# A two-layer decoder trunk on one core: rotary sine product a step later, first swaps by ScalarE, raw weights asked for later, scores of two query blocks in one bank each

## The chip, the cores and the metric

The kernel runs on one core of a Trainium2 chip. The metric is the device time of one execution in microseconds (us); the time before the change is the median of three runs, 1908.89 us (1908.52 to 1911.45).

## What is computed

Two layers, each of the same form, on 512 positions of width 1024; all weights are float32 and are read from HBM once:

```
h    = modulate(rmsnorm(x, norm_mix_g), sh_m, sc_m)          # sh, sc, g come from c by w_ada
proj = h @ w_in                                              # a_in, b_in, q, k, v, gate_pre
a    = silu(layernorm(conv31(glu(a_in))));  y_a = a @ w_a_out
y_b  = (bg * conv3(cg * xb)) @ w_b_out
q, k = rope(q), rope(k)        # [t1*cos - t2*sin, t2*cos + t1*sin] on halves of 32 of a head part of 64
for each of 8 heads, each block of 128 queries, both parts c of q and k:
    p_c = softmax(mask(q_c @ k_c.T * scale));   a = p_0 - lam * p_1;   o = a @ v
y_c  = rmsnorm(o, subln_g) * (1 - lambda_init) @ w_c_out
x    = x + g_m * ((sigmoid(gates) * (y_a, y_b, y_c) summed) @ w_out)
x    = x + g_f * (square(relu(modulate(rmsnorm(x), sh_f, sc_f) @ w_ff1)) @ w_ff2)
out  = rmsnorm(x, final_g)
```

## The kernel before

**Products.** Every float32 product is done as three reduced-precision products: an operand is split into a high part (ScalarE's cast, L394 for weights) and the rest (VectorE's subtraction, L402), and `proj` (L426) adds high*high, high*rest and rest*high in one PSUM bank. A product of 128 output columns has 24 matmuls of 512 columns.

**Order.** The program order of all engines is written by hand. `mm` (L143) counts the columns that TensorE has been given, and each 4096 columns are a **step**. Side work is written as generators: `spawn(g, d)` starts one d steps later, and `yield n` lets n steps go by, so the number of a step says only where in each engine's stream an instruction stands. Each engine then goes through its own stream in order and waits where its data aren't there. Tasks that are due in one step run in the order in which they were put off (the earlier first).

**Weights.** A raw tile is 1024 rows by 256 columns, 1 MB, and there are two of them (`wraw`, two buffers). `raw_issue` (L365) asks for the next one on SP's queue. `w_split` (L373) turns half a raw tile, a chunk, into high and rest: the cast, one step later the subtraction, and after a second half at once the next `raw_issue`. `release` starts the split of the chunk three ahead one step after a product has used its own chunk. In the attention part the chunks of a pair of heads come as q first half, k first half, q second half, k second half, then the two halves of v (each four row blocks by 256 columns).

**Rotary.** `rope` (L707): ScalarE copies the product from PSUM to an SBUF tile `t` (L712), four DMAs on SP's queue copy the four groups of 32 partitions to `sw` with neighbours swapped (L714), one step later VectorE multiplies by the cosine (L717), two steps after that it multiplies `sw` by the sine and adds (L719, L720); a step later ScalarE casts (L723, L724), a step later VectorE makes the rests (L728, L729 for q; L734 for k) and SP moves halves between partitions (L738, L739); two steps later the tile counts as there.

**Attention.** `heads` (inside `mixer`) starts a head every nine steps, the first when its q and k count as there and two steps have gone by. `attend` (L780) writes the scores of one query block every two steps. Both parts of a block have a PSUM bank of their own (`ps_s`, two banks in all), 128 to 512 columns in use. `softmax` (L745): a step later VectorE's masked minimum reads both banks (L754), a step later ScalarE's exponentials (L761), two steps later VectorE's combination (L766, L767, L770). Five steps after the last block TensorE transposes the weights (L806), in three portions a step apart, four steps after the last of them it multiplies by v (L817); then come ScalarE's copy (L821), a step later transposes of it (L825), and four small steps of the norm with a row broadcast (L455) and a multiplication by VectorE (L842).

**Where the steps fall.** Let V be the step at which the value products of one pair of heads end. The four q and k products of the next pair end at V+3, V+6, V+9 and V+12, its value products at V+18. Two casts of weights stand at V+4 (second halves of q and k), with their subtractions and the two requests for raw tiles (v of this pair, q of the next) at V+5; the cast of the first half of v stands at V+7, its subtraction at V+8. In layer 0 the even head's four blocks stand at V+1, V+3, V+5 and V+7, the odd head's from V+10 on; in layer 1 both two steps earlier. The tables of the sine and cosine are ready before the first product ends.

**The layers' first tiles.** In layer 0 the four products of the first pair are made by hand at the end of the list `START` (`first_product`), in layer 1 three of the four in `closing`, in the banks of `ps_mm` and `ps_s`. `lambdas` (L228) makes lam with small instructions; its product on TensorE (L251) stands two steps after VectorE's difference (L246).

Of the kernel before, what the change touches and what calls it, by code (L numbers as in the profile page):

```python
# [44 lines left out]
ADA_BR = 0  # L45
FIRST = 2
RWAIT = 2


RDELAY = (0, 1, 1)  # L50
# [17 lines left out]
SH_M, SC_M, G_M, SH_F, SC_F, G_F = range(6)  # L68
# [3 lines left out]
def kernel(  # L72
# [7 lines left out]
    nc = tc.nc  # L80
# [23 lines left out]
    def ftile(dt=F32, shape=None):  # L104
        return slot("f", dt, shape)
# [4 lines left out]
    def ps_s():  # L110
        return psum.tile([P, S], F32, tag="s", name=nm("s"), bufs=2)
# [119 lines left out]
    def lambdas():  # L231
        lq, lk = slot("at", F32, [1, L, 2, 64]), slot("at", F32, [1, L, 2, 64])
        for j, (a, b) in enumerate(((lam_q1, lam_k1), (lam_q2, lam_k2))):
            G.dma_start(lq[:, :, j, :], a[None, :, :])
            G.dma_start(lk[:, :, j, :], b[None, :, :])
        yield 15
        V.tensor_tensor(lq, lq, lk, op=ALU.mult)
        ls, le, ll = stile(4), stile(4), stile(2)
        V.tensor_reduce(out=ls[0:1, :], in_=lq.rearrange("p l j d -> p (l j) d"), op=ALU.add, axis=AX.X)
        ones = ftile(F32, [1, P])  # L240
        V.memset(ones, 1.0)
        yield 1
        A.activation(le[0:1, :], ls[0:1, :], AF.Exp)
        yield 1
        for l in range(L):
            V.scalar_tensor_tensor(  # L246
                out=ll[0:1, l : l + 1], in0=le[0:1, 2 * l + 1 : 2 * l + 2], scalar=-lam_init[l],
                in1=le[0:1, 2 * l : 2 * l + 1], op0=ALU.add, op1=ALU.subtract)
        yield 2
        pt = ps_t()  # L250
        T.matmul(pt[:, 0:2], ones, ll[0:1, :], start=True, stop=True)  # L251
        yield 1
        V.tensor_copy(nlam, pt[:, 0:2])
        written.add("lam")
# [103 lines left out]
            chunks += [(len(specs) + g, hh) for hh in range(2) for g in range(len(grp))]  # L358
            specs += grp
    raws, wready = [], []  # L360
    wnext, spare = [0], set()

    def raw_issue():
        if len(raws) < len(specs):
# [6 lines left out]
    def w_split(extra=None):  # L371


        if wnext[0] >= len(chunks):
            return
        n, hh = chunks[wnext[0]]
        wnext[0] += 1
        raw, kk = raws[n], specs[n][2]
        if kk < 0:

            shape, rs = [P, 4, 256], raw[:, 4 * hh : 4 * hh + 4, :]
            n_k = 4
        else:
            shape, rs = [P, 8, P], raw[:, :kk, hh * P : (hh + 1) * P]
            n_k = kk
        if extra:
            half = [P, n_k // 2] + shape[2:]
            his = [slot(extra, F32R, half) for _ in range(2)]
            parts = [(hf, rs[:, i * half[1] : (i + 1) * half[1], :]) for i, hf in enumerate(his)]
        else:  # L390
            hi = wpool.tile(shape, F32R, tag="wh", name=nm("wh"))
            parts = [(hi[:, :n_k, :], rs)]
        for h_, r_ in parts:
            A.copy(h_, r_)  # L394
        yield 1
        if extra:
            los = [slot(extra, F32R, half) for _ in range(2)]
        else:
            lo = wpool.tile(shape, F32R, tag="wl", name=nm("wl"))
            los = [lo[:, :n_k, :]]  # L400
        for l_, (h_, r_) in zip(los, parts):
            V.tensor_tensor(l_, r_, h_.bitcast(F32), op=ALU.subtract)  # L402
        wready.append(([h_[:, k, :] for h_, _ in parts for k in range(n_k // len(parts))],
                       [l_[:, k, :] for l_ in los for k in range(n_k // len(parts))], extra))
        if hh == 1:
            raw_issue()

    def getw():
# [295 lines left out]
    cos_t = const.tile([P, S], F32, name="cos_t")  # L704
    sin_t = const.tile([P, S], F32, name="sin_t")

    def rope(pp, res, j):  # L707

        t, sw = ftile(), ftile()
        A.copy(t, pp)  # L712
        for q in range(4):
            nc.sync.dma_start(sw[32 * q : 32 * q + 32, :], t[32 * (q ^ 1) : 32 * (q ^ 1) + 32, :])  # L714
        yield 1
        u = ftile()
        V.tensor_tensor(u, t, cos_t, op=ALU.mult)  # L717
        yield 2
        V.tensor_tensor(sw, sw, sin_t, op=ALU.mult)  # L719
        V.tensor_tensor(u, u, sw, op=ALU.add)  # L720
        yield 1
        d0, d1 = slot("qk", F32R), slot("qk", F32R)
        A.copy(d0, u)  # L723
        A.copy(d1[64:, :], u[64:, :])  # L724
        yield 1
        if j % 2 == 0:
            e0, e1 = slot("qk", F32R), slot("qk", F32R)
            V.tensor_tensor(e0, u, d0.bitcast(F32), op=ALU.subtract)  # L728
            V.tensor_tensor(e1[64:, :], u[64:, :], d1[64:, :].bitcast(F32), op=ALU.subtract)  # L729
            moves = ((d0, d0, d1, d1), (e0, e0, e1, e1))  # L730
            parts = (d0, d1, e0, e1)
        else:
            lo = u.bitcast(F32R)
            V.tensor_tensor(lo, u, d0.bitcast(F32), op=ALU.subtract)  # L734
            moves = ((d0, u, d1, u),)
            parts = (d0, d1)
        for a0, b0, a1, b1 in moves:
            nc.sync.dma_start(a0[64:, :].bitcast(F32), b0[:64, :].bitcast(F32))  # L738
            nc.sync.dma_start(a1[:64, :].bitcast(F32), b1[64:, :].bitcast(F32))  # L739
        yield RWAIT  # L740
        res.append(parts)
# [38 lines left out]
    def attend(l, hd, q, k, v, res):  # L780

        a = []
        l0 = stile(4)
        for i in range(NTB):
            n = (i + 1) * P
            sps = [ps_s(), ps_s()]
            blk = slice(i * P, (i + 1) * P)
            for cc in range(2):
                T.matmul(sps[cc][:, :n], q[cc][:, blk], k[cc][:, :n], start=True, stop=False)  # L789
                T.matmul(sps[cc][:, :n], q[2 + cc][:, blk], k[cc][:, :n], start=False, stop=True)  # L790
            spawn(softmax(l, i, sps, l0, a))
            yield QSTEP
        yield AWAIT

        tiles = [None] * NTB
        for js in ((0,), (1, 3), (2,)):
            pt = ps_t()
            off = 0
            hi, lo = slot("at", F32R) if js[0] < 2 else None, slot("at", F32R)
            w2 = 2 * P  # L800
            if js[0] == 2:
                hi, lo = lo[:, :w2], lo[:, w2:]
            for j in js:
                w = S - j * P
                for i in range(j, NTB):
                    T.transpose(pt[:, off + (i - j) * P : off + (i - j + 1) * P],  # L806
                                a[i][:, j * P : (j + 1) * P], ident)
                tiles[j] = (hi[:, off : off + w], lo[:, off : off + w])
                off += w
            spawn(weights_t(pt, off, hi, lo))  # L810
            yield 1
        yield PWAIT
        po = ps_t()
        for j in range(NTB):
            for i, (x_, y_) in enumerate(PASSES):
                c0 = j % 2 * 256 + hd % 2 * P
                T.matmul(po[:, j * P :], v[j // 2][x_][:, c0 : c0 + P], tiles[j][y_],  # L817
                         start=j == 0 and i == 0, stop=j == NTB - 1 and i == 2)
        yield 1
        of = slot("o")  # L820
        A.copy(of, po)  # L821
        yield 1
        pt = ps_t()
        for b in range(NTB):
            T.transpose(pt[:, b * P : (b + 1) * P], of[:, b * P : (b + 1) * P], ident)  # L825
        yield 1
        ss = stile(4)
        for b in range(NTB):
            A.activation(pt[:, b * P : (b + 1) * P], pt[:, b * P : (b + 1) * P], AF.Square,
                         scale=128.0**-0.5, accum_out=ss[:, b : b + 1])  # L830
        yield 4

        e = stile(4)
        G.tensor_tensor(e, l0, l0, op=ALU.mult)
        G.tensor_scalar(out=e, in0=e, scalar1=EPS, scalar2=None, op0=ALU.mult)
        G.tensor_tensor(e, e, ss, op=ALU.add)
        y = rsqrt_small(e, 4)
        yield 2
        rb = bcast(y, 4)
        yield 1  # L840
        assert (l, "sub") in written
        V.scalar_tensor_tensor(out=of, in0=of, scalar=subg[:, l : l + 1], in1=rb,  # L842
                               op0=ALU.mult, op1=ALU.mult)
        res[hd] = of


    def mixer(l, h, qk, nfirst):
# [15 lines left out]
                yield PERIOD  # L863

        spawn(heads())
        for hp in range(NH // 2):
            if hp:
                qk, nfirst = [], 0
# [162 lines left out]
        def branch(pp, br, e, tg):  # L1031
# [6 lines left out]
            else:  # L1038
# [2 lines left out]
                yield 1  # L1041
                yield from split(m[e], merged)

        for br, act in enumerate((oo, yb, ya)):
            hold[0] = False
            if br == ADA_BR and l == 0:
# [121 lines left out]
    h = new_h()  # L1168
# [111 lines left out]
    def first_product(qt, i):  # L1280
# [6 lines left out]
        proj(first[i], w1[i], h, 0, S, 2 * qt, 2 * qt + 2)  # L1287
        if qt == 3:
            release(w1[i])
            spawn(rope(first[i], qk, i))  # L1290
            run_due()

    def rows_scale(qt):
# [35 lines left out]
    for l in range(L):  # L1329
# [6 lines left out]
        f = mlp(l, h, f, NF)  # L1336
        if l + 1 < L:
            qk = []
            h = closing(l, G_F, f, l + 1, 0, lambda pp, i: rope(pp, qk, i))
    ending(f)  # L1340
    while tasks:
        step()
# [35 lines left out]
```

## Time and profile before

| | us |
|---|---|
| median of 3 runs | 1908.89 |
| lowest and highest | 1908.52, 1911.45 |
| profiled execution | 1904.28 |
| its span, first to last instruction | 1902.5 |

The profiled execution thus has 1.8 us around its span and is 4.6 us under the median of the runs. Its mean granted TensorE clock is 0.997 of full. The profile is one execution: for each instruction its engine, line, start and length, the idle time of the engine before it, and what ended that. A tile `raw` is a raw weight tile, `wh` and `wl` are high and rest of a chunk, `s` a bank of scores, `t` another small PSUM bank, `f` and `st` small SBUF tiles, `cv` (in this part) the softmax tiles. A DMA row on SP's queue (`SPq`) is the issue, not the transfer.

### The profile page before, as it was taken

To read this page: it belongs to the slowest core of one execution; us is meant where nothing else is said; L and a number is where in the kernel's file an instruction comes from. 1 tells how busy PE (TensorE), PEld (TensorE's weight loads), DVE (VectorE), ACT (ScalarE), POOL (GpSimd) and SP (SyncE) were. 2 spreads that over 40 slices of the span, in tenths; PEclk is the share of its full clock that TensorE was granted. 3 is DMA by queue.
4 is the path that set the end of the run, shared out by engine and by line. 5 is a ranking of instruction groups with operands and counts; after the bars stand their busy time and mean duration, and the time that the engine had idled before them with its cause. 6 is when DMAs were issued, how large, how long until landed. Compare 5 with 4: busy or idle time off the path is not lost.

```text
span 1902.5 us, 24972 instructions
## 1 busy us (share of the span) xinstructions
PE 1874.3 (99%) x9565; PEld 1599.9 (84%) x9565; DVE 1256.0 (66%) x2139; ACT 785.8 (41%) x1420; POOL 63.4 (3%) x109
## 2 busy tenths in 40 slices
PE   8999999999999999999999999999999999999998
PEld 6788888888889888888898888888888898888888
DVE  7788789996676556565677777898654563333336
ACT  4466652223333524333445666322243353424253
POOL 1011010000000000000000000000000000000000
PEclk9999999999999999999999999999999999999999
DMA  8644323444554455555535442232233422223221
GB/s 272 181 130 126 101 67 98 151 138 145 166 178 135 139 178 195 177 185 182 171 97 142 123 122 73 89 104 96 67 100 100 133 89 89 89 93 106 89 89 67
DMA packets 211527, 241.20 MB, mean 127 GB/s; under 512 B 10408, under 2 KB 178480, under 8 KB 211408
## 3 DMA queue, kind: packets, MB, share of 16 engines
q1 hardware_dynamic: 210480, 239.38, 40.6%
q8 instruction: 75, 1.23, 0.3%
q0 software_dynamic: 768, 0.23, 0.1%
q14 instruction: 44, 0.36, 0.1%
q10 hardware_dynamic: 160, 0.01, 0.0%
HBM read 216.50 MB, written 2.10 MB: 115 GB/s over the span
## 4 chain that ended last, share of the span: by engine, by line
PE 93%; DMA 3%; DVE 2%; issue 1%; SPq 1%; ACT 1%; POOL 0%; POOLq 0%; DVEq 0%; ACTq 0%
PE mm L145 83%; PE s L145 3%; DMA f<-f 2%; PE t L817 1%; PE s L789 1%; PE s L790 1%; PE t L806 1%; SPq L714 1%; PE t L1193 1%; PE t L455 0%; PE t L303 0%; PE t L825 0%; POOL st L438 0%; DVE f L719 0%; PE t L1214 0%
## 5 line engine op out<-in xcount | busy, mean ns | idle before, releaser
L145 PE MATMUL mm<-h,wh 128*128 128x512 f32 x2720 | 851.3, 392 | 0.0
L145 PEld LDWEIGHTS mm<-h,wh 128*128 128x128 f32 x2720 | 509.6, 188 | 103.3
L145 PE MATMUL mm<-h,wl 128*128 128x512 f32 x1360 | 533.6, 392 | 0.0
L394 ACT CAST wh<-raw 128x1024 fp32r<-128x1024 f32 (+1 forms) x308 | 308.9, 1005 | 407.2 <-PE mm L145 358.2
L402 DVE TENSOR_TENSOR wl<-raw,wh 128x1024 fp32r<-128x1024 f32 (+1 forms) x308 | 358.2, 1166 | 69.6 <-ACT wh L394 65.9
L145 PE MATMUL mm<-qk,wh 128*128 128x512 f32 (+1 forms) x1024 | 300.2, 376 | 0.0
L145 PEld LDWEIGHTS mm<-h,wl 128*128 128x128 f32 x1360 | 256.2, 188 | 51.9
L145 PEld LDWEIGHTS mm<-qk,wh 128*128 128x128 f32 x1024 | 188.2, 188 | 35.1
L145 PE MATMUL mm<-qk,wl 128*128 128x512 f32 (+1 forms) x512 | 192.6, 376 | 0.0
L912 DVE SCALAR_TENSOR_TENSOR cv<-v,caw,cv 128x511 f32<-128x511 f32 (+14 forms) x240 | 176.0, 733 | 4.2
L499 DVE SCALAR_TENSOR_TENSOR xT<-mm,ada,xT 128x512 f32<-128x512 f32 (+1 forms) x81 | 56.0, 691 | 151.2 <-PE mm L145 151.0
L281 DVE SCALAR_TENSOR_TENSOR araw<-araw,cact,araw 128x512 f32<-128x512 f32 x140 | 104.6, 747 | 25.2 <-DMA araw<-in_w_ada_dram 24.7
L145 PEld LDWEIGHTS mm<-qk,wl 128*128 128x128 f32 x512 | 96.3, 188 | 17.2
L1059 ACT ACTIVATE f<-mm 128x512 f32<-128x512 f32 x60 | 35.9, 598 | 160.6 <-PE mm L145 160.6
L145 PE MATMUL mm<-o,wh 128*128 128x512 f32 (+1 forms) x320 | 95.5, 381 | 0.0
L145 PE MATMUL mm<-v,wh 128*128 128x512 f32 (+1 forms) x320 | 94.9, 379 | 0.0
L145 PE MATMUL mm<-wh,h 128*128 128x256 f32 x448 | 84.1, 284 | 0.0
L761 ACT ACTIVATE cv<-cv,st 128x128 f32<-128x128 f32 (+3 forms) x128 | 71.0, 558 | 25.6 <-DVE st L754 25.2
L1033 DVE SCALAR_TENSOR_TENSOR f<-f,mm 128x512 f32<-128x512 f32 x38 | 26.1, 687 | 83.6 <-PE mm L145 83.6
L469 DVE TENSOR_TENSOR qk<-f,qk 128x512 fp32r<-128x512 f32 x38 | 26.3, 691 | 77.4 <-ACT qk L466 77.2
L438 POOL TENSOR_TENSOR st<-st,nhalf 128x4 f32<-128x4 f32 (+2 forms) x29 | 31.2, 1076 | 1368.0 <-DVE st L460 1013.4
L145 PEld LDWEIGHTS mm<-wh,h 128*128 128x128 f32 x448 | 70.8, 191 | 0.4
(259 smaller groups left out, 2282.9 us busy)
## 6 DMA issues: line engine op xcount, KB each, us to landing
raw<-in_w_in_dram SPq DMA_DIRECT2D x66, 1024.0 KB, 5.2
raw<-in_w_ff_dram SPq DMA_DIRECT2D x64, 1024.0 KB, 5.4
araw<-in_w_ada_dram SPq DMA_DIRECT2D x160, 256.0 KB, 3.0
f<-f SPq DMA_DIRECT2D x128, 64.0 KB, 2.0
qk<-qk SPq DMA_DIRECT2D x64, 128.0 KB, 2.6
raw<-in_w_c_out_dram SPq DMA_DIRECT2D x8, 1024.0 KB, 5.0
raw<-in_w_out_dram SPq DMA_DIRECT2D x8, 1024.0 KB, 5.0
qk<-in_w_ada_dram SPq DMA_DIRECT2D x16, 256.0 KB, 6.0
```

Source lines behind the costliest of these rows:

```text
L145: T.matmul(ps, lhsT, rhs, start=start, stop=stop)
L281: V.scalar_tensor_tensor(out=part, in0=r, scalar=cact[:, k : k + 1], in1=part, op0=ALU.mult, op1=ALU.add)
L394: A.copy(h_, r_)
L402: V.tensor_tensor(l_, r_, h_.bitcast(F32), op=ALU.subtract)
L438: G.tensor_tensor(y, v[:, :n], nhalf[:, :n], op=ALU.pow)
L469: V.tensor_tensor(lo, src, hi.bitcast(F32), op=ALU.subtract)
L499: V.scalar_tensor_tensor(out=xT[e][:, t0:t1], in0=pp[:, t0:t1], scalar=g[:, e : e + 1], in1=xT[e][:, t0:t1], op0=ALU.mult, op1=ALU.add)
L714: nc.sync.dma_start(sw[32 * q : 32 * q + 32, :], t[32 * (q ^ 1) : 32 * (q ^ 1) + 32, :])
L761: A.activation(p[cc][:, :n], p[cc][:, :n], AF.Exp, bias=nb[:, cc : cc + 1], scale=-1.0, accum_out=l0[:, i : i + 1] if cc == 0 else s1)
L912: V.scalar_tensor_tensor(out=ac[:, s:], in0=glu[j][:, : S - s], scalar=wk, in1=ac[:, s:], op0=ALU.mult, op1=ALU.add)
L1033: V.scalar_tensor_tensor(out=t, in0=t, scalar=1.0, in1=pp, op0=ALU.add, op1=ALU.mult)
L1059: A.activation(r, pp, AF.Relu)
```

## The change

`rope` gets a flag `near`. With it, ScalarE makes the swap itself, by four copies of 32 partitions from the PSUM bank into `sw`; no SBUF copy `t` is made, no swap DMAs are issued, VectorE's cosine product reads the PSUM bank, and the sine product stands one step after the cosine product. The first four tiles of layer 0 and the three of `closing` in layer 1 use it. All other tiles keep the DMAs, and their sine product stands three steps after the cosine product and no longer two.

In `mixer`, from the start of the heads to the start of the branches, `w_split` lets two steps go by after a second half's subtraction before it asks for the next raw tile.

`attend` writes both parts of the blocks of 128 and 256 columns into one bank, beside each other; the blocks of 384 and 512 columns keep two banks.

In `lambdas` the product on TensorE stands four steps after VectorE's difference and no longer two.

```diff
+SWAIT = 3
+RAWD = 2
...
-        yield 2
+        yield 4
         pt = ps_t()
         T.matmul(pt[:, 0:2], ones, ll[0:1, :], start=True, stop=True)
...
         if hh == 1:
+            if rdelay[0]:
+                yield rdelay[0]
             raw_issue()
...
-    def rope(pp, res, j):
-        t, sw = ftile(), ftile()
-        A.copy(t, pp)
-        for q in range(4):
-            nc.sync.dma_start(sw[32 * q : 32 * q + 32, :], t[32 * (q ^ 1) : 32 * (q ^ 1) + 32, :])
+    def rope(pp, res, j, near=False):
+        sw = ftile()
+        if near:
+            t = pp
+            for q in range(4):
+                A.copy(sw[32 * q : 32 * q + 32, :], pp[32 * (q ^ 1) : 32 * (q ^ 1) + 32, :])
+        else:
+            t = ftile()
+            A.copy(t, pp)
+            for q in range(4):
+                nc.sync.dma_start(sw[32 * q : 32 * q + 32, :], t[32 * (q ^ 1) : 32 * (q ^ 1) + 32, :])
         yield 1
         u = ftile()
         V.tensor_tensor(u, t, cos_t, op=ALU.mult)
-        yield 2
+        yield 1 if near else SWAIT
...
-            sps = [ps_s(), ps_s()]
+            sps = [ps_s()]
+            sps.append(ps_s() if n > 256 else sps[0][:, n:])
...
         spawn(heads())
+        rdelay[0] = RAWD
...
+        rdelay[0] = 0
         for br, act in enumerate((oo, yb, ya)):
...
-            spawn(rope(first[i], qk, i))
+            spawn(rope(first[i], qk, i, True))
...
-            h = closing(l, G_F, f, l + 1, 0, lambda pp, i: rope(pp, qk, i))
+            h = closing(l, G_F, f, l + 1, 0, lambda pp, i: rope(pp, qk, i, True))
```

More of the change, by code (lines that the diff above doesn't have):

```diff
@@ L360 @@
     raws, wready = [], []
-    wnext, spare = [0], set()
+    wnext, spare, rdelay = [0], set(), [0]
     def raw_issue():
```

## The prediction

> **What bounds the kernel now.** I read the page first.
>
> ```profile
> span 1902.5 us, 24972 instructions
> PE 1874.3 (99%) x9565; PEld 1599.9 (84%) x9565; DVE 1256.0 (66%) x2139; ACT 785.8 (41%) x1420; POOL 63.4 (3%) x109
> ```
>
> TensorE is busy 99% of the span and the change takes no product away, so only its waits can be won or added. All the time that this change can touch stands in TensorE's own waits and, for each, in the timeline:
>
> ```profile
> PE t L251 <- DVE st L246: 0.8, 1, 0.8
> ```
> ```profile
> 76.10 0.30 PE L789 MATMUL s<-qk,qk 128*128 128x128 f32 x1 [3.19 <-DMA qk<-f]
> 102.90 0.39 PE L789 MATMUL s<-qk,qk 128*128 128x256 f32 x1 [1.07 <-DVE st L754]
> 113.49 0.50 PE L789 MATMUL s<-qk,qk 128*128 128x512 f32 x1 [0.68 <-DVE st L754]
> 1028.02 0.39 PE L789 MATMUL s<-qk,qk 128*128 128x256 f32 x1 [2.16 <-DVE st L754]
> 1032.93 0.62 PE L145 MATMUL mm<-h,wh 128*128 128x512 f32 x2
> 1033.39 0.39 PE L145 MATMUL mm<-h,wl 128*128 128x512 f32 x1
> 1075.89 0.39 PE L789 MATMUL s<-qk,qk 128*128 128x256 f32 x1 [0.57 <-DVE st L754]
> 1123.55 0.39 PE L789 MATMUL s<-qk,qk 128*128 128x256 f32 x1 [1.10 <-DVE st L754]
> ```
>
> A matmul row is 0.39 long, but a second one adds only 0.23 (0.62 for two); so an idle time in brackets is a delay of 0.16 more, and a step of eight such matmuls is 1.84. The five waits for VectorE come to 1.23 + 0.84 + 2.32 + 0.73 + 1.26 = 6.4. Four of them stand before a block of 256 columns: the second block of a head waits until VectorE has read the first out of the same two banks. Long waits cost more than their length:
>
> ```profile
> 1028.60:1031.90 3.30, 3.30 (x11) 2.45 (x10) 1.85 (x3) 2.75 (x7) 0.43 (x2) 0.53 0.44 97
> 1124.00:1127.00 3.00, 3.00 (x20) 2.60 (x19) 2.12 (x4) 2.90 (x12) 0.00 (x0) 1.00 0.38 87
> ```
>
> In these windows (after the duration PE, PEld, DVE, ACT and POOL with counts, then the granted clock) the clock is 0.53 for 3.3 us after the wait of 2.16, which loses 3.3 x 0.47 = 1.5; after the wait of 1.10 it is 1.00. The wait at 76.10 is longer still, and I give it 1.5 too. Why VectorE is late shows the chain of waits:
>
> ```profile
> 1020.23 5.99 DMA f<-f
> ```
>
> The swap of a rotary tile took 6 us, since two raw tiles had been asked for ahead of it on the same queue, and the sine product stood in VectorE's order ahead of the minimum that TensorE waited for.
>
> **The change part by part, in the attention part.** *One bank for two parts* takes away the second block's wait for the first: the next that meets a bank in use is the third block, a step after the second's minimum. *The sine product a step later* and *raw tiles behind the swaps* take away VectorE's wait for the swap. With these alone the five waits and the cooling go: 6.4 + 1.5 = 7.9 won.
>
> But the first half of v is cast at V+7, and the tile it is cast from is now asked for in that very step. I follow it from ScalarE's copy of the second product (V+6), in layer 0's third pair:
>
> ```profile
> 134.95 0.59 ACT L712 COPY f<-mm 128x512 f32<-128x512 f32 x1 [1.48 <-PE mm L145]
> 137.94 1.03 ACT L394 CAST wh<-raw 128x1024 fp32r<-128x1024 f32 x1
> 140.87 0.72 ACT L761 ACTIVATE cv<-cv,st 128x512 f32<-128x512 f32 x1 [1.90 <-DVE st L754]
> 142.31 0.56 ACT L712 COPY f<-mm 128x512 f32<-128x512 f32 x1
> ```
> ```profile
> 130.72 2.10 SPq L367 DMA_DIRECT2D raw<-in_w_in_dram  x2
> 135.56 2.41 SPq L714 DMA_DIRECT2D f<-f  x4
> ```
> ```profile
> DMA to landing us min/median/max: 5.1/5.2/9.8
> ```
>
> Now the request goes out at 130.72, lands about 135.9, and the cast at 137.94 does not wait. Afterwards it stands behind the four swap issues, which end 135.56 + 2.41 - 134.95 = 3.0 after the copy's start; 5.2 later, at 8.25, the tile is there. The cast ends 0.95 after that, at 9.2, where it now starts at 3.0: ScalarE stands still for some 5 us, and behind it stand, at V+8, two rotary casts and the exponentials (142.31 - 140.87 = 1.4, both parts), or the copy L821. Then VectorE:
>
> ```profile
> 139.00 1.23 DVE L402 TENSOR_TENSOR wl<-raw,wh 128x1024 fp32r<-128x1024 f32 x1 [0.59 <-ACT wh L394]
> 142.88 0.69 DVE L719 TENSOR_TENSOR f<-f,sin_t 128x512 f32<-128x512 f32 x1 [0.44 <-DMA f<-f]
> 144.81 0.15 DVE L766 RECIPROCAL st<-st 128x1 f32<-128x1 f32 x1
> 145.93 0.74 DVE L842 SCALAR_TENSOR_TENSOR o<-o,subg,t 128x512 f32<-128x512 f32 x1
> ```
>
> The rest of v's half (V+8) waits for the cast and ends at 9.3 + 1.2 = 10.5. In VectorE's order follow two rotary rests (V+9; two operations like L719, 1.4, to 11.9; ScalarE's casts are done at 9.2 + 1.3 = 10.5, its exponentials at 11.9), sine product and sum of the second tile (V+10, 1.4, to 13.3) and the combination of the even head's last block (V+10; 145.93 - 144.81 = 1.1, to 14.4). TensorE wants that for its transposes. Layer 0's heads stand a step earlier than now, because the first tiles count as there a step earlier, so the transposes come at V+11 and no longer V+12:
>
> ```profile
> 101.23 0.60 PE L806 MATMUL t<-ident,cv 128*128 128x128 f32 x4
> 149.38 0.60 PE L806 MATMUL t<-ident,cv 128*128 128x128 f32 x4
> ```
> ```profile
> 89.07 0.59 ACT L712 COPY f<-mm 128x512 f32<-128x512 f32 x1 [3.27 <-PE mm L145]
> ```
>
> Third pair: 149.38 - 134.95 - 1.84 = 12.6 after the copy, so a wait of 14.4 - 12.6 = 1.8; the fourth pair has the same work, 1.8. Second pair, where no earlier head is in its later stages: 101.23 - 89.07 - 1.84 = 10.3, a wait of 4.1, and 1.5 for the clock.
>
> ```profile
> 1017.79 0.59 ACT L712 COPY f<-mm 128x512 f32<-128x512 f32 x1 [3.39 <-issue]
> 1064.84 0.59 ACT L712 COPY f<-mm 128x512 f32<-128x512 f32 x1 [3.36 <-PE mm L145]
> ```
> ```profile
> 1025.26 0.60 PE L806 MATMUL t<-ident,cv 128*128 128x128 f32 x4
> 1076.46 0.60 PE L825 MATMUL t<-ident,o 128*128 128x128 f32 x4
> ```
>
> In layer 1 heads stand two steps earlier and the last block is combined in time; late are the odd head's minima (V+8, V+10). Second pair: VectorE is through with the rest of v at 10.5, the first block's minimum at 10.9, rests at 12.3, sine at 13.7, the second's minimum at 14.4; TensorE reaches the third block two steps after transposes that move to 1025.26 - 1.84 - 1017.79 = 5.6, with some 1.4 of transposes and scores between: 10.7, a wait of 3.7, and 1.5. Third and fourth pair: the transposes L825 need ScalarE's copy L821 (V+8), there at 9.2 + 0.6 = 9.8, and come at 1076.46 - 1064.84 - 0.73 - 1.84 = 9.05: 0.75 each.
>
> Added: 4.1 + 1.5 + 1.8 + 1.8 + 3.7 + 1.5 + 0.75 + 0.75 = 15.9, against 7.9 won: +8.0. Bounds per pair: below, nothing, if what stands behind the cast has slack that I don't see; above, a step more each, 1.84.
>
> **The layers' starts.**
>
> ```profile
> 53.87 0.59 ACT L712 COPY f<-mm 128x512 f32<-128x512 f32 x1 [2.83 <-PE mm L145]
> 54.35 1.14 ACT L394 CAST cv<-raw 128x512 fp32r<-128x512 f32 x2
> 65.61 1.05 ACT L394 CAST wh<-raw 128x1024 fp32r<-128x1024 f32 x1 [3.54 <-DMA raw<-in_w_in_dram]
> 67.04 0.62 ACT L723 CAST qk<-f 128x512 fp32r<-128x512 f32 x1
> 67.68 0.62 ACT L724 CAST qk<-f 64x512 fp32r<-64x512 f32 x1
> ```
> ```profile
> 54.48 5.29 SPq L714 DMA_DIRECT2D f<-f  x8
> 59.87 0.53 SPq L367 DMA_DIRECT2D raw<-in_w_in_dram  x1
> 73.25 0.46 SPq L738 DMA_DIRECT2D qk<-f  x1
> ```
>
> Layer 0: sixteen swap issues leave SP's queue, but the request at 59.87 hardly moves, since the subtraction that frees its buffer ends about then; ScalarE still waits for it until about 65.4. A copy of 32 partitions has no row; casts of 128 and of 64 partitions both take 0.62, so I take a full copy's spacing, 0.48 (54.35 - 53.87), for each, and as lower bound a quarter. Three more copies for each of four tiles are 5.8 on ScalarE, of which 4.3 fit in waits (2.1 before 59, 3.5 before 65.61 less the request's gain), while q's casts now come ahead of the cast that waits. k's casts end at 69.6 about as now, its rest at 70.6 (VectorE no longer has the fourth tile's sine ahead of it), its moves go out at 70.6 and land 76.1 - 73.25 = 2.8 later or less, at 73.2. TensorE is there at 70.2: a step earlier (72.9 - 1.84) and without the wait L251 of 0.9. It waits 3.0, with 1.5 for the clock: 4.5 against 3.35 + 1.5 + 0.9 = 5.75, 1.3 won; with quick copies up to 3 more, with k's casts a tile later 2 less. Layer 1: the k tile's moves no longer stand behind swaps, and a wait of 0.3 there goes. Banks held longer by these tiles are wanted only after the scores; nothing else waits for them.
>
> Sum: 8.0 - 1.3 - 0.3 = +6.4. On the profiled execution's 1904.28 that is 1910.7, on the median of the runs (4.6 higher) 1908.89 + 6.4 = 1915.3.
>
> Two rules of the Trainium skill speak to this. The row at 1028.02 has a wait of 2.16 with half the clock behind it. "TensorE: Matmul & The Clock Gate" (Part 1) says that the clock falls back after at least one idle window of about 3.4 us; by that the waits of 3.0 to 4.1 here need not cool it, and the sum would be up to 4.5 less; the measured row decides. "PSUM — Partial Sum Buffer" (PSUM bank collisions) says that no two engines may use one bank's quadrant at once, two readers included; then ScalarE's four copies and VectorE's cosine product take turns, and a minimum waits for the second part in its bank: an estimate of 0.2 to 0.7 more at the start. No row here shows either order.
>
> **The rivals.** *The cast's wait stays off TensorE (faster).* VectorE is busy 66% and ScalarE 41%, so a stop of 5 us may be caught up. Then 7.9 + 1.3 + 0.3 = 9.5 are won: 1899.4. It decides if the results due at V+8 to V+10 have over 4 us of slack; the rows above give 10.3 to 12.6 for work that ends at 14.4, which speaks against it. *The stop costs, but less (no change).* If the rests or the sine product don't stand ahead of what TensorE wants (1.4 each, two of them), the waits shrink to 1.3, 0, 0, 0.9, 0.75, 0.75 without cooling, 3.7: -5.8, 1903.1, which counts with the faster case; if only one of them doesn't, to 2.7 + 1.5, 0.4, 0.4, 2.3 + 1.5, 0.75, 0.75 = 10.3: +0.8, 1909.7. *ScalarE's extra copies are late for k (slower by 2 more)*: in the upper bound.
>
> **How the numbers follow.** A measurement of this kernel tells some 0.2% (3.8 us) from no change. I give the forecast (five waits replaced by six longer ones) 0.47, the middle case 0.22, full gain or near it 0.31. So faster 0.31, same 0.22, slower 0.47. The forecast's own range is 1911 to 1921 (half a step less or more on the four longer waits, the start's bounds); the range over the cases is 1898 to 1921, below to a little past the full gain.
>
> **What would show it.** Right: the cast L394 at V+7 (near 92, 138, 184, 1021, 1068, 1115) waits some 5 us for `raw`; VectorE's L402 behind it waits too; TensorE waits at L806 in layer 0 (about 4, 2, 2), at L789 with 384 columns in layer 1's second pair, at L825 after; no wait at L789 with 256 columns, none at L251, none of L719 for a swap. Wrong: that cast waits, but TensorE's waits after it stay under 1 us; or the first scores come without a wait.

## The result, and the profile after

The changed kernel took 1923.39 us (median of 4 runs, 1922.02 to 1923.95), the kernel before 1908.70 in the same comparison (1904.95 to 1911.45): a ratio of 1.0086, 95% interval 1.0074 to 1.0098. It is 14.7 slower by the medians, where 6.4 had been forecast. The sign and the place were right, the size was not: the time lies above the range. The profiled executions differ by 1921.6 - 1902.5 = 19.1 in their spans.

First TensorE's waits in the changed kernel (total, times, longest), then the busy times on its page:

```profile
PE t L818 <- DVE cv L781: 8.5, 3, 4.2
PE s L801 <- DVE st L765: 5.4, 2, 2.9
PE t L837 <- ACT o L833: 4.6, 2, 2.8
PE s L801 <- issue: 3.7, 1, 3.7
```
```profile
PE 1879.9 (98%) x9565; PEld 1604.2 (83%) x9565; DVE 1255.8 (65%) x2139; ACT 794.9 (41%) x1441; POOL 62.3 (3%) x109
```

Lines have moved: L818 is the transposes of the weights (L806 before), L801 the scores (L789), L837 the transposes of o (L825), L781 the combination (L770), L765 the minimum (L754), L404 the rest (L402), L396 the cast (L394). The five waits at blocks of 256 columns are gone, and so is L251's. In their place stand seven, at the three lines that the prediction named. ScalarE's timeline shows the cause, the cast of the first half of v (start, length, in brackets the idle time before it); a copy of the second product goes ahead of each (two of these copies are shown):

```profile
90.42 0.57 ACT L723 COPY f<-mm 128x512 f32<-128x512 f32 x1
98.94 1.05 ACT L396 CAST wh<-raw 128x1024 fp32r<-128x1024 f32 x1 [7.96 <-DMA raw<-in_w_in_dram]
149.07 1.05 ACT L396 CAST wh<-raw 128x1024 fp32r<-128x1024 f32 x1 [7.92 <-DMA raw<-in_w_in_dram]
198.49 1.05 ACT L396 CAST wh<-raw 128x1024 fp32r<-128x1024 f32 x1 [8.75 <-DMA raw<-in_w_in_dram]
1028.59 0.57 ACT L723 COPY f<-mm 128x512 f32<-128x512 f32 x1
1038.53 1.04 ACT L396 CAST wh<-raw 128x1024 fp32r<-128x1024 f32 x1 [9.37 <-DMA raw<-in_w_in_dram]
1089.28 1.04 ACT L396 CAST wh<-raw 128x1024 fp32r<-128x1024 f32 x1 [9.11 <-DMA raw<-in_w_in_dram]
1138.87 1.04 ACT L396 CAST wh<-raw 128x1024 fp32r<-128x1024 f32 x1 [8.12 <-DMA raw<-in_w_in_dram]
```

Six casts, in pairs 2 to 4 of both layers, stand still until their tile lands. VectorE and TensorE follow (layer 0's second pair first, then TensorE's other six waits):

```profile
100.02 1.23 DVE L404 TENSOR_TENSOR wl<-raw,wh 128x1024 fp32r<-128x1024 f32 x1 [5.24 <-ACT wh L396]
105.19 0.48 PE L818 MATMUL t<-ident,cv 128*128 128x128 f32 x1 [4.22 <-DVE cv L781]
```
```profile
155.32 0.33 PE L818 MATMUL t<-ident,cv 128*128 128x128 f32 x1 [1.77 <-DVE cv L781]
204.74 0.33 PE L818 MATMUL t<-ident,cv 128*128 128x128 f32 x1 [2.50 <-DVE cv L781]
1041.31 0.44 PE L801 MATMUL s<-qk,qk 128*128 128x384 f32 x1 [2.51 <-DVE st L765]
1044.77 0.69 PE L801 MATMUL s<-qk,qk 128*128 128x384 f32 x1 [2.85 <-DVE st L765]
1090.86 1.12 PE L837 MATMUL t<-ident,o 128*128 128x128 f32 x4 [2.78 <-ACT o L833]
1140.45 0.66 PE L837 MATMUL t<-ident,o 128*128 128x128 f32 x4 [1.79 <-ACT o L833]
```

The brackets come to 18.4; with 0.16 each, as in the prediction, 19.5. The clock adds to that (after the stretch: its length, busy times of PE, PEld, DVE, ACT, POOL, the granted clock, and the transfers):

```profile
103.86:107.27 3.41, 2.08 (x8) 1.89 (x9) 3.34 (x11) 2.77 (x8) 0.00 (x0) 0.50 0.74 163
107.27:110.68 3.41, 3.41 (x12) 2.72 (x11) 2.38 (x8) 0.71 (x2) 0.48 (x1) 0.50 0.44 97
202.84:206.25 3.41, 1.51 (x11) 1.47 (x12) 3.31 (x11) 3.12 (x7) 0.00 (x0) 1.00 0.79 175
206.25:209.66 3.41, 3.41 (x24) 3.05 (x24) 3.38 (x9) 3.32 (x15) 1.24 (x2) 1.00 0.27 62
1042.53:1045.94 3.41, 1.17 (x5) 1.08 (x5) 3.27 (x11) 3.23 (x7) 0.77 (x2) 0.50 0.78 172
1045.94:1049.35 3.41, 3.41 (x10) 2.70 (x9) 3.41 (x6) 1.22 (x4) 0.00 (x0) 0.50 0.25 59
1086.90:1090.31 3.41, 1.18 (x10) 0.88 (x8) 0.00 (x0) 1.03 (x2) 0.00 (x0) 1.00 1.02 329
1090.31:1093.72 3.41, 2.86 (x9) 2.48 (x10) 3.30 (x8) 3.33 (x12) 0.00 (x0) 0.50 0.06 18
```

Three times TensorE was put on half clock: during the wait of 4.22, during that of 2.85 (which stands two matmuls behind that of 2.51) and at the end of that of 2.78; with those of 2.50, 1.77 and 1.79 it kept the full clock. In the five windows at 0.50 it worked for 2.08 + 3.41 + 1.17 + 3.41 + 2.86 = 12.9 us, and half of that, about 6.5, is lost. Waits and clock come to about 26; the spans of the changed kernel and of the same kernel without the delay (the first experiment) differ by 25.5.

### The profile page after: what moved, and what is told of

It reads as the page before. It is cut to its first block, busy times and chain, and to the rows that moved or that the text cites. A ratio compares the mean times of both kernels' runs of the same rounds, so it can differ in the third digit from the quotient of the medians.

```text
span 1921.6 us, 24916 instructions
## 1 busy us (share of the span) xinstructions
PE 1879.9 (98%) x9565; PEld 1604.2 (83%) x9565; DVE 1255.8 (65%) x2139; ACT 794.9 (41%) x1441; POOL 62.3 (3%) x109
## 4 chain that ended last, share of the span: by engine, by line
PE 90%; DVE 3%; ACT 3%; DMA 2%; issue 1%; POOL 0%; POOLq 0%; DVEq 0%; ACTq 0%
PE mm L147 81%; PE s L147 3%; DMA raw<-in_w_in_dram 2%; PE t L829 1%; ACT wh L396 1%; PE s L801 1%; PE t L818 1%; PE s L802 1%; PE t L1207 1%; DVE cv L765 1%; DVE wl L404 1%; PE t L305 0%; ACT f L720 0%; PE t L459 0%; PE t L837 0%
## 5 line engine op out<-in xcount | busy, mean ns | idle before, releaser
L396 ACT CAST wh<-raw 128x1024 fp32r<-128x1024 f32 (+1 forms) x308 | 309.3, 1005 | 451.0 <-PE mm L147 355.9
L404 DVE TENSOR_TENSOR wl<-raw,wh 128x1024 fp32r<-128x1024 f32 (+1 forms) x308 | 358.4, 1166 | 94.3 <-ACT wh L396 91.2
L765 DVE CUSTOM_DVE_ANT_0 cv<-s,mask 128x128 f32<-128x128 f32 (+3 forms) x128 | 57.3, 485 | 25.1 <-PE s L802 25.1
```

Source lines behind the costliest of these rows:

```text
L765: V.tensor_tensor_reduce(out=pp[:, :n], in0=sps[cc][:, :n], in1=mask[:, S - n :], op0=ALU.add, op1=ALU.min, scale=-0.125, scalar=3.0e38, a ...
```

## The experiments

The theory after the result: **the loss is the cast's stop**, since its tile is asked for behind the swaps on SP's queue, and all else in the change wins some 8. The rivals: the loss comes from heads that stand a step earlier, or from ScalarE's narrow copies. In the expectations theory 1 is the first, theory 2 a rival. Ratios are to the kernel before, with 95% intervals, each from five rounds; the medians of the kernel before were 1906.5 to 1907.2 in these.

| kernel | us | ratio |
|---|---|---|
| changed, no delay | 1898.94 | 0.9962 (0.9948 to 0.9975) |
| changed, delay of one step | 1897.70 | 0.9958 (0.9946 to 0.9971) |
| changed, only the second tile delayed | 1898.29 | 0.9960 (0.9947 to 0.9972) |
| before, delay alone | 1937.61 | 1.0166 (1.0152 to 1.0180) |
| changed, without the copies | 1931.34 | 1.0140 (1.0122 to 1.0157) |
| changed, neither delay nor copies | 1898.52 | 0.9957 (0.9945 to 0.9970) |
| before, later sine product alone | 1897.06 | 0.9955 (0.9941 to 0.9969) |
| before, packed banks alone | 1904.41 | 0.9987 (0.9977 to 0.9997) |
| before, copies alone | 1905.56 | 0.9994 (0.9985 to 1.0002) |
| changed, no delay, copies for two tiles | 1904.92 | 0.9992 (0.9980 to 1.0003) |
| before, swaps on GpSimd's queue | 1903.69 | 0.9986 (0.9977 to 0.9995) |
| later sine product, first swaps on GpSimd's queue | 1897.18 | 0.9950 (0.9937 to 0.9964) |

### The delay taken out of the change

```diff
-RAWD = 2
+RAWD = 0
```

> The changed kernel with the raw tiles asked for at once (as in the kernel before); all its other parts stay. Theory 1 (the loss is the cast of v's first half, which stands still on ScalarE for some 8 us because its tile is asked for behind the swaps): its six stops go, and with them TensorE's waits of 4.2, 1.8 and 2.5 at the transposes of layer 0, of 2.5 and 2.9 at the third block of layer 1's second pair and of 2.8 and 1.8 behind the copy of o, with the half clock after three of them some 24 us; the five waits of before stay away, VectorE waits for a swap again, but under 1 us each. Time 1900 (1897 to 1904). Theory 2 (the loss comes from layer 0's and layer 1's heads standing a step earlier, so that TensorE asks too early whatever the cast does): waits at the transposes remain, 1912 or more.

1898.94, as theory 1 had it. TensorE's waits from the attention part that are left:

```profile
PE s L801 <- issue: 3.7, 1, 3.7
```
```profile
PE t L818 <- DVE at L789: 0.8, 1, 0.8
```

All seven waits went with this one number. One detail of theory 1 failed: VectorE's waits for a swap come to 6.0, the longest 2.9, and not to under 1 each. The delay costs 1923.39 - 1898.94 = 24.5 in the changed kernel, and the rest of the change wins 0.4%.

### The delay alone, and the delay without the copies

The first puts the two lines of the delay into the kernel before. The second undoes the copies in the changed kernel:

```diff
-        if near:
-            t = pp
-            ...
-        else:
-            t = ftile()
+        t = ftile()
...
-        yield 1 if near else SWAIT
+        yield 2 if near else SWAIT
```

> The kernel before with the raw tiles asked for two steps later and nothing else changed. Theory 1: the cast stands still for 7 to 9 us in pairs 2 to 4 of both layers as in the changed kernel; TensorE's waits at the transposes and behind the copy of o are a step (1.8) shorter, since the heads stand a step later, and the waits for a minimum in a bank get longer; time 1913 to 1921. Theory 2: the cast's stop is covered, 1909 within 3.

> The changed kernel with the first tiles of a layer swapped by the DMA queue again (sine product two steps after the cosine product there, as before), so that the heads of both layers stand a step later again; the delay of the raw tiles stays. Theory 1: the cast's six stops stay as long as they are, but TensorE's waits behind them are up to a step (1.8) shorter each: 8 to 11 us of the loss go, and the start of layer 0 gives 0.5 back; time 1912 to 1917. Theory 2: nearly the whole loss goes, 1900 to 1904. If neither the copies nor the step matter: 1923.

Both came out dearer than either theory said: 1937.6 and 1931.3. With the delay alone TensorE waits 13.8 for minima (nine times) and 8.8 for combinations (three times). That the loss is the delay's holds, but my reason for expecting less was wrong: a head that stands a step later has no more slack. In the kernel without copies the order of VectorE and then TensorE, at the place where the changed kernel waited for a combination, is this:

```profile
99.73 1.23 DVE L404 TENSOR_TENSOR wl<-raw,wh 128x1024 fp32r<-128x1024 f32 x1 [7.96 <-ACT wh L396]
100.87 0.69 DVE L760 CUSTOM_DVE_ANT_0 cv<-s,mask 128x512 f32<-128x512 f32 x1
```
```profile
101.62 0.48 PE L796 MATMUL s<-qk,qk 128*128 128x128 f32 x1 [3.51 <-DVE st L760]
```

The even head's last minimum (L760 here) now stands behind the rest that waits; in the changed kernel the same minimum is done at 91.89, ahead of it:

```profile
91.89 0.68 DVE L765 CUSTOM_DVE_ANT_0 cv<-s,mask 128x512 f32<-128x512 f32 x1
```

TensorE wants the minimum's bank sooner than it wants the combination. The second reason lies in layer 1's first pair, where the changed kernel has no swap issues ahead of the request on SP's queue. Here the request goes out at 1010.44, and a seventh cast stops:

```profile
1016.45 1.04 ACT L396 CAST wh<-raw 128x1024 fp32r<-128x1024 f32 x1 [5.04 <-DMA raw<-in_w_in_dram]
```
```profile
1018.26 0.30 PE L796 MATMUL s<-qk,qk 128*128 128x128 f32 x1 [2.50 <-DMA qk<-f]
```

TensorE's wait there is not for the cast but for k's moves. They were issued from 1013.76 on, 3.3 after the raw tile, and landed 4.4 and 4.2 later; in the changed kernel the request stands 4.8 ahead of them, and they land in 2.2 and 2.4. So the delay also costs through what lands behind the tile.

### The later place in the queue, or the later step?

One kernel has `RAWD = 1`; the other delays the second of a pair's two requests alone (`if rdelay[0] and n % 3 == 1`), so that the tile which the cast reads is asked for at once.

> The changed kernel with the raw tiles asked for one step later in the program, not two. On SP's queue the two requests of a pair then stand where they stand without a delay, behind the swap issues of the first tile and ahead of those of the second; the request for v's tile alone stands a few issues later. Theory 1 (what counts is the place in SP's queue, since SP runs ahead of the steps): no stop of the cast, time as with no delay, 1899 (1897 to 1901). Rival (each step of delay makes the request a step, 1.8, later): half of the loss is there, some 1911.

> The changed kernel, with only the second of the two raw tiles of a pair's q and k asked for two steps later; the first (the one that the cast of v's first half reads) and v's own are asked for at once. Theory 1: the cast no longer waits, the swaps of the second tile stand behind one raw tile and not two, VectorE waits for none of them; time 1899 (1896 to 1903), the same as with no delay or up to 2 faster. Rival (the second tile is late in its turn for the next cast, and the stop only moves on): 1905 or more.

Both times are as theory 1 had them: 1897.70 and 1898.29, with no stop of 7 to 9 us. A step of delay costs nothing by itself: SP works ahead of the steps, and with one step the two requests stand at the same place of its queue as with none, ahead of the second tile's swap issues (layer 0's second pair):

```profile
86.10 1.95 SPq L369 DMA_DIRECT2D raw<-in_w_in_dram  x2
89.96 2.42 SPq L725 DMA_DIRECT2D f<-f  x4
```

Two steps put them behind these four swap issues, which wait for ScalarE's copy. That with only the second tile delayed the swaps stand behind one raw tile and not two brought nothing that the intervals can tell; VectorE, which was to wait for none of them, still waited 4.9 (two times).

### Neither delay nor copies

> The changed kernel with neither the delay of the raw tiles nor the narrow copies: the later sine product, the packed banks and lambda's product stay. Theory 1 (packing adds nothing to the later sine product; heads that stand a step earlier only help where the cast stops, since their minima are through before it): 1897 (1895 to 1899) as with the sine product alone, so that the delay costs 31 to 36 without the copies and 24.5 with them. Rival (packing has its own price: the third block meets the first's bank): 1900 or more.

1898.52. So the delay costs 1931.34 - 1898.52 = 32.8 without the copies and 24.5 with them: they win nothing by themselves, but they move the minima out of the stop's way and spare the wait in layer 1's first pair. What each of the two is worth was not separated.

### Which part wins: sine product, packing or copies

```diff
-        yield 2
+        yield 3
         V.tensor_tensor(sw, sw, sin_t, op=ALU.mult)
```

(That of the sine product, with lambda's product two steps later; a layer's first tiles keep two steps. Packing and copies as in the change, each into the kernel before, the copies with lambda's product too.)

> The kernel before with the sine product a step later in pairs 2 to 4 (and lambda's product two steps later, as in the change); no packing, no narrow copies, no delay of the raw tiles. Theory 1 (the waits at blocks of 256 columns come from VectorE standing before the sine product until the swap lands): VectorE's waits of 2.0 to 2.6 for a swap fall under 0.8, TensorE's five waits of 6.4 in sum and the cooling of 1.5 go nearly, lambda's 0.9 too: 1900 (1898 to 1903). Rival (the second block waits for the first's bank whatever VectorE does): 1906 or more.

> The kernel before with the two parts of a block of 128 or 256 columns in one bank, nothing else changed. Theory 1: VectorE still waits for the swaps, but what meets a bank in use is the third block, a step (1.8) later than the second; the waits of 1.23, 0.84, 0.73 and 1.26 go and that of 2.3 falls to 0.5 with no cooling: 1901 (1899 to 1904), so that this part and the sine product win the same time and not the sum. Rival (what VectorE has late is then waited for at the transposes or at the third block): 1905 or more.

> The kernel before with the narrow copies for the first tiles (heads a step earlier) and lambda's product two steps later; no packing, the sine product two steps after the cosine product as before, no delay. Theory 1 (VectorE still stands before the sine product until the swap lands; with the heads a step earlier their first minimum is in VectorE's order ahead of it more often): the start is even with before, lambda's wait of 0.9 goes, of the five waits about half: 1903 (1900 to 1906). Rival (TensorE asks a step earlier for the same late minima): the waits grow by up to 1.8 each, 1909 to 1914.

The sine product with lambda's product gives 0.9955, the whole gain, a little more than I expected. No run has the one without the other; lambda's wait was 0.9 before, and the copies, which have lambda's product too, gained nothing that shows. VectorE's order shows why the sine product counts, in layer 1's second pair:

```profile
1023.37 0.29 DVE L760 CUSTOM_DVE_ANT_0 cv<-s,mask 128x128 f32<-128x128 f32 x1
```
```profile
1024.45 0.69 DVE L725 TENSOR_TENSOR f<-f,sin_t 128x512 f32<-128x512 f32 x1 [0.57 <-DMA f<-f]
```

The minimum is through ahead of the sine product, which before came first (at 1026.34, with the minimum at 1027.67). VectorE still waits for swaps, 6.2 in all against 13.5, the longest 2.1 where under 0.8 was expected:

```profile
DVE f L725 <- DMA f<-f: 6.2, 9, 2.1
```

but nothing that TensorE wants stands behind it. Packing alone came out between the two theories, with its rival's picture: the wait is at the third block, of 384 columns, and longer than the one it replaces (2.16).

```profile
1035.11 0.69 PE L790 MATMUL s<-qk,qk 128*128 128x384 f32 x1 [3.27 <-DVE st L754]
```

The copies alone make no difference that can be told. Theory 1 had about half of the waits left, and one of 3.44 at layer 1's start outweighs the others:

```profile
1007.84 0.39 PE L800 MATMUL s<-qk,qk 128*128 128x256 f32 x1 [3.44 <-DVE st L765]
```

### Does another queue free the swaps?

```diff
-            nc.sync.dma_start(sw[32 * q : 32 * q + 32, :], t[...])
+            nc.gpsimd.dma_start(sw[32 * q : 32 * q + 32, :], t[...])
```

> The kernel before with the rotary swaps issued on GpSimd's queue instead of SP's, nothing else changed. Theory 1 (a swap lands late because it stands behind two raw tiles on the same queue): swaps land in 2 to 2.5 after their issue, VectorE's waits of 2.0 to 2.6 at the sine product go, TensorE's waits at blocks of 256 columns too: 1898 (1896 to 1901). Rival (the raw tiles hold the sixteen DMA engines whatever queue the swap comes from): swaps still land 5 to 6 after, 1905 or more.

Theory 1 fell, and the rival's time (1905 or more) wasn't met either. The place is that of the prediction's swap of 6 us: the two requests on SP's queue, then the issue on GpSimd's and VectorE's sine product:

```profile
1014.08 1.51 SPq L367 DMA_DIRECT2D raw<-in_w_in_dram  x2
```
```profile
1017.98 1.97 POOL L714 DMA_DIRECT2D f<-f  x4 [5.12 <-ACT f L712]
```
```profile
1027.01 0.69 DVE L719 TENSOR_TENSOR f<-f,sin_t 128x512 f32<-128x512 f32 x1 [3.30 <-DMA f<-f]
```

Issued from 1017.98 on, the swap is there at 1027.0, 9 us later, on a queue of its own (the page lists it as a software queue, the raw tiles as a hardware one). Both raw tiles had been asked for by 1014.08 + 1.51 = 1015.6. So the swap doesn't overtake the large transfer by another queue. The four parts landed 7.4 to 8.1 after their issues, and at the same place on SP's queue 6.0 to 7.2. GpSimd's queue isn't slow by itself: the median of all its swaps is 2.3, of SP's 2.0. The prediction's "on the same queue" is thus no condition for the swap to be late; that the raw tiles make it late, by whichever queue it goes, fits. "DMA: Bandwidth & Descriptors" of the Trainium skill (Queues, rings and completion order) says both that an engine goes round robin between queues, by which one would hope for more, and that a semaphore's write lands only after all earlier writes of that engine, across its queues. The trace agrees with the second as far as it goes; it doesn't show the order inside an engine. The time was 0.1% less all the same: TensorE's waits for minima grew (8.5 against 5.6), but at layer 0's start it no longer waits for k's moves (3.2 before). How these make up the time was not followed further.

### Layer 0's start

> The changed kernel with no delay of the raw tiles, and with ScalarE's four narrow copies only for the first two tiles of a layer; the third and the fourth are swapped by the queue, sine product two steps after the cosine product as before. Theory 1 (at layer 0's start TensorE's wait of 3.9 and the half clock after it, 2 more, come from ScalarE: sixteen narrow copies of 0.59 each stand ahead of k's casts): eight copies of 0.59 become two, ScalarE is some 3.5 earlier at k's casts, the moves land as much earlier, and the wait falls below 1 with no cooling: 4 to 6 less than no delay, 1893 to 1895. Rival (k's moves stand behind the eight swap issues on SP's queue instead): no gain, 1898 to 1900.

> The kernel with the later sine product alone, and the swaps of a layer's first four tiles issued on GpSimd's queue; the others stay on SP's. Theory 1 (at layer 0's start k's moves, ready at 71.5, are issued at 74.1 because sixteen swap issues and q's moves stand ahead of them on SP's queue): they go out 2 to 2.5 earlier, TensorE's wait of 5.0 before the first scores falls to about 3 and its cooling shrinks: 1894 (1892 to 1896). Rival (ScalarE's cast of k after the raw tile is the limit): no change, 1897.

Both theories 1 failed. With copies for two tiles only, layer 0's wait stays (3.9 against 3.7): SP's queue spends 7.35 on eight swap issues ahead of the moves, as the rival had it. But 6 us of the gain are lost, more than the rival said, and they are lost at layer 1's start, in a wait that it had not had:

```profile
62.27 7.35 SPq L725 DMA_DIRECT2D f<-f  x8
```
```profile
1004.66 0.44 PE L801 MATMUL s<-qk,qk 128*128 128x128 f32 x1 [4.92 <-issue]
```

There the request for a raw tile goes out right ahead of k's moves (997.31 and 998.28); the one whose landing the trace has came 6.4 after its issue. With no delay and copies for all first tiles the request stands 4.8 ahead, and the moves land in 2.2 and 2.4.

With the first swaps on GpSimd's queue the wait at layer 0's start fell from 5.0 to 4.1, and the time stayed at 1897.2.

```profile
PE s L795 <- DMA qk<-f: 4.1, 1, 4.1
```

SP issued k's moves at 73.72, right behind q's and only 0.4 earlier than with all swaps on SP; what limits them then was not tried further. The later sine product (with lambda's product), 0.45% faster than the kernel before and, by the two ratios, 1.3% faster than the changed one, is the simplest of the best.

## Why the prediction was right in sign and wrong in size

**What bounds the kernel** held: the differences lie in TensorE's waits and its clock, and in no busy time.

**The gain of the other parts.** 9.5 was forecast (7.9 + 1.3 + 0.3); 0.38% of 1907.07 is 7.2, by the intervals 4.8 to 9.9, and the spans give 1902.5 - 1896.1 = 6.4. The sum was near, in part by luck, for its division was not: packing and sine product were given 7.9 together, and the sine product (with lambda's product) has all of it, while the 1.3 of layer 0's start did not come. The step "the next that meets a bank in use is the third block, a step after" took it for granted that the third block finds the bank free.

**Layer 0's start** was to win 1.3 and won nothing that shows. Narrow copies were set at 0.48 each, and they take 0.59, as long as copies of four times the partitions; twelve more are 7.1 and not 5.8:

```profile
67.81 2.35 ACT L720 COPY f<-mm 32x512 f32<-32x512 f32 x4
```
```profile
72.24 0.46 SPq L749 DMA_DIRECT2D qk<-f  x1
```
```profile
74.52 0.44 PE L801 MATMUL s<-qk,qk 128*128 128x128 f32 x1 [3.71 <-issue]
```

k's moves went out at 72.24 and not 70.6, and the first scores came at 74.5 and not 73.2; a step ahead of where they stood before would be 76.10 - 1.84 = 74.3. The half clock there was given 1.5; it lasted 6.8 us here and 3.4 in the same kernel without the delay, so its price at this place varies.

**The delay: this is the step that failed**, and by its size. Added were to be 15.9 (12.9 of waits, 3.0 of clock); it is 24.5 to 25.5 (the rows give 19.5 and about 6.5). Its places came out as written, but for two waits of VectorE for a swap (4.5 in all) where none was forecast. In layer 0 waits of 4.1, 1.8 and 1.8 were forecast and 4.4, 1.9 and 2.7 came (with the 0.16). In layer 1 forecast were 3.7, 0.75 and 0.75, and 5.7, 2.9 and 1.95 came. Three terms were off.

First the landing. "5.2 later, at 8.25, the tile is there" took the median of all raw tiles. The rows are these:

```profile
1029.18 2.41 SPq L725 DMA_DIRECT2D f<-f  x4
1031.69 1.18 SPq L369 DMA_DIRECT2D raw<-in_w_in_dram  x2
```

The cast started 1038.53 - 1031.69 = 6.8 after the first request, and 9.9 after the copy. From copy to cast the six places, in order of time, have 8.5, 8.5, 9.3, 9.9, 9.7 and 8.7, which is 5.2 in sum above the forecast; TensorE's waits behind them grew by 0.3, 0.1, 0.9, 2.0, 2.2 and 1.2, 6.6 in sum. So most of the missing wait goes with the landing. The swap issues ended 3.1 after the copy each time, where 3.0 was forecast; from the request to the cast it is 5.4 to 6.8. All six have two tiles asked for back to back, so this doesn't tell the long landings from the short, and what does stays open. (The longest landing that the prediction quotes, 9.8, is that of a second tile of such a pair; the first ones landed in 5.1 to 6.3 in the kernel before.)

Second TensorE's arrival, counted from ScalarE's copy. In layer 1 that copy was not the free zero point I took it for; it stands right behind the exponentials of the even head's last block:

```profile
1078.90 0.71 ACT L772 ACTIVATE cv<-cv,st 128x512 f32<-128x512 f32 x1
1079.60 0.56 ACT L723 COPY f<-mm 128x512 f32<-128x512 f32 x1
```

TensorE was ready for the transposes of o at 1090.86 - 2.78 = 1088.1, 8.5 after the copy where 9.05 was forecast. Landing (1.4) and arrival (0.6) together turn 0.75 into 2.75; the row has 2.78, or 2.94 with the 0.16. These two are read from the rows; that no kernel held the one and changed the other leaves their shares argued.

Third the clock, which was to cost 3.0 and cost about 6.5. The prediction gave each cooled wait 3.3 us at half clock; here it lasted 6.8, 6.8 and 3.4. "TensorE: Matmul & The Clock Gate" (Part 1) of the Trainium skill names at least one idle window of about 3.4 us. The traces agree with the window, not with its being idle throughout. In all fourteen kept traces, from 50 us on, the clock changes only on a grid of 3.41 us, whose position differs from trace to trace. After each of the 35 windows at full clock in which TensorE was idle for 2.03 us or more, the next window is at half clock; after those idle for less than 1.66 none is; between 1.67 and 1.93 both occur. So it matters how a wait falls on the grid: that of 2.78 put 2.23 of idle time into one window (1086.90, with 1.18 busy), that of 2.50 was shared out and the fuller window had 1.90 (202.84, with 1.51 busy).

**The rivals.** That the stop doesn't reach TensorE, or costs less, is refuted by the seven waits. Of what the forecast said about one PSUM bank read by two engines, the trace shows that VectorE's cosine product waited for ScalarE's copies twice, 4.9 in all; what that cost was not separated. The range ended at half a step per wait, and left out that all waits of a layer could grow together for one reason, the late landing.

## What to carry to other kernels

A hand-written step says where an instruction stands in a queue, not when it runs: before a request is moved, look at what it will stand behind and who reads the tile next, and let the range of a landing, not its median alone, go into the bounds. When an engine stops, count what stands behind the stop in each engine's order, for what TensorE wants soonest decides much of the loss: the same delay cost 24.5 with the minima ahead of the stop and 32.8 with one behind it and k's moves behind a raw tile. And time each part of a change alone: here two small ones, the sine product with lambda's product, had the whole gain, and another lost some three times as much.

## What the hardware showed that I had not expected

A 64 KB swap on another engine's queue landed no sooner behind the 1 MB tiles (9 us from first issue to use, 8 on SP's). ScalarE's copy of 32 partitions by 512 takes 0.59, the same as one of 128 partitions. Of waits between 2.1 and 2.9 us some bring half clock (2.16, 2.78) and some don't (2.50): in these traces the idle time within a window of a 3.41 us grid tells, and half clock comes in whole windows of it.
